# Transposes of two feature tiles' probabilities one step sooner in each half of the attention

## The chip, the cores and the metric

The kernel runs on one core of one Trainium2 chip. The metric is the device time of one execution in microseconds (us), as the median over several executions.

## What is computed

A decoder block for 256 tokens of width 1024, in float32. One normalised input is projected by `w_in` into seven parts; two gated mixers run side by side, a causal gMLP mixer (`y_a`) and an attention with 16 heads of 64 (`y_b`); they are merged, projected and added to the input. Two more stages follow, a squared-ReLU MLP and a gate on per-layer embeddings. With 256 tokens there is one block of keys, so the attention is plain causal attention with a bias by distance. Cut to what matters:

```python
h = rms_norm(x, norm_mix_g)
za_u, za_v, q, k, v_att, g_a, g_b = jnp.split(h @ w_in, offsets, axis=-1)
y_a = sgu_mixer(jax.nn.gelu(za_u), jax.nn.gelu(za_v), w_sgu_spatial, b_sgu_spatial, ln_v_g, ln_v_b)
y_b = moba_attention(heads(q), heads(k), heads(v_att), rel_bias)   # softmax(q k^T / 8 + bias, causal) @ v
merged = jax.nn.sigmoid(g_a) * y_a + jax.nn.sigmoid(g_b) * y_b
x = x + merged @ w_out
x = x + jnp.square(jax.nn.relu(rms_norm(x, norm_ffn_g) @ w_ff1)) @ w_ff2
x = x + jax.nn.sigmoid(rms_norm(x, norm_ple_g) @ w_ple_gate) * (p @ w_ple_proj)
return rms_norm(x, norm_final_g)
```

## The kernel before

**Weights.** All weights come as 1 MB tiles (128 x 2048) in one fixed order, through four buffers (`raw`). ScalarE rounds each tile into a high part `hi` (L85), VectorE takes the rest as a low part `lo` (L86), and TensorE multiplies the parts. Both parts have three buffers. A tile is split two tiles ahead of its use, and the load of a tile waits until the low part of the tile four before it has been taken.

**Attention, in two halves.** The features are worked on in eight feature tiles of 128 (two heads each), numbered `c` = 0 to 7; each half `J` of a Python loop handles four of them, in two pairs `a` and `b`. The order of the instructions on every engine is the order in which the code is written (a manual schedule); nothing is moved by a planner. One half runs through: `keys(a)`, `keys(b)` with the scores of the first two feature tiles in its middle, `att_normalise` of these two, the value projection `w_va` and the gate projection `gate_a`, into which the transposes (`att_transpose`) and the value products (`value_two`) of the first two feature tiles and the scores and softmax of the third and fourth (`score_two`) are put as extra work. Then come `att_normalise` for the third and fourth, `gate_b(a)`, `merge_b(a)`, `gate_b(b)`, `merge(a)`. The value products of the third and fourth feature tile are made one stage later: in the middle of `keys` of the second half (`values_b(1)`), and after the first twelve matmuls of the output projection (`values_b(3)`).

**The lines at stake.** `att_transpose(c)` puts six transposes of the normalised probabilities `s` on TensorE (L428), written into the PSUM tile `sp` in which the scores had been, and one ScalarE copy of all six to SBUF, `pt` (L429). `att_values(c)` multiplies `pt` with the values into the one PSUM buffer `yb` (L440, L442). `gate_b(j)` is a projection of two PSUM tiles, each of 16 matmuls (L215, L217) and followed by a ScalarE copy (L229); then VectorE adds two halves (L232) and scales (L473), and ScalarE takes the tanh `tb` (L475). Its optional `mid` is extra work that is issued after the first PSUM tile's copy. `merge(j)` transposes four blocks of `u` (L485), and VectorE and ScalarE write the merged features `mT` (L486, L108, L109).

**PSUM.** The `sp` tiles have two buffers of two banks each. After the loop that pool is closed, and the four accumulators `o` of the output projection take its place (L121, L123, L124: 12 matmuls for each 128 rows of `w_out`, six for each half of the columns). So the first matmul of the output projection has to wait until the last `sp` tile has been read, which the copy L429 of feature tile 7 does. In the built program that first matmul waits for ScalarE alone, and the count that it waits for is that of this copy.

Of the kernel before, what the change touches and what calls it, by code (L numbers as in the profile page):

```python
# [51 lines left out]
def block_kernel(ctx: ExitStack, tc: tile.TileContext, xt, xk, pt, rows, wst, bsp, rel, buckets, wts, out):  # L52
# [43 lines left out]
    def weights(key, width, ahead=3):  # L96
        i = POS[key]
        split_to(i + ahead)
        k = 2048 // width
        return (hi[i].rearrange("p (k c) -> p k c", k=k), lo[i].rearrange("p (k c) -> p k c", k=k))  # L100
# [28 lines left out]
    def bank(tag="mm", bufs=3, shape=(P, 2, 256)):  # L129
        return ps.tile(list(shape), F32, tag=tag, name=f"{tag}_t", bufs=bufs)  # L130
# [77 lines left out]
    def two_rows(R):  # L208
        return R[:, None, :].to_broadcast([P, 2, S])

    def wide_mm(o, wh, wl, x, f, ks):

        fs = slice(f * P, (f + 1) * P)
        for k in ks:
            nc.tensor.matmul(o, wh[:, k, fs], x[:, k], start=k == 0, stop=False, skip_group_check=True)  # L215
        for k in ks:
            nc.tensor.matmul(o[:, 0], wl[:, k, fs], x[:, k, 0], start=False, stop=k == KD - 1, skip_group_check=True)  # L217

    def wide_out(name):
        return act.tile([P, 2, 2, S], F32, tag="ln", name=name, bufs=2)  # L220

    def proj_T(key, x, mid=None):

        wh, wl = weights(key, CW)
        z = wide_out(f"z_{key[0]}{key[1]}")
        for f in range(2):
            o = bank()
            wide_mm(o, wh, wl, x, f, range(KD))
            nc.scalar.activation(z[:, f], o, AF.Copy)  # L229
            if f == 0 and mid:  # L230
                mid()
        nc.vector.tensor_add(z[:, :, 0], z[:, :, 0], z[:, :, 1])  # L232
        return z[:, :, 0]

    def proj_tok(name, c, post, mids={}):


        os_ = [bank(shape=(P, 512)) for t in range(2)]
        for i in range(2):
            wh, wl = weights((name, 2 * c + i), 512)  # L240
            for t in range(2):
                ts = slice(t * P, (t + 1) * P)
                for k in range(4):
                    kk = 4 * i + k
                    nc.tensor.matmul(os_[t], xg2[:, kk, 0, ts], wh[:, k], start=kk == 0, stop=False)  # L245
                    nc.tensor.matmul(os_[t], xg2[:, kk, 0, ts], wl[:, k], start=False, stop=False)  # L246
                    nc.tensor.matmul(os_[t], xg2[:, kk, 1, ts], wh[:, k], start=False, stop=kk == KD - 1)  # L247
                if i:
                    post(t, os_[t])
                for f in mids.get(2 * i + t, ()):  # L250
                    f()
# [82 lines left out]
    def by_token(dst, c, func):  # L334
        def post(t, o):
            nc.scalar.activation(dst[:, t, halves(c)], o, func, scale=r0[:, t:t + 1])
        return post
# [74 lines left out]
    def att_normalise(c):  # L412
        s, sm = sc_sb[c]
        rc = small.tile([P, 2, 2], F32, tag="rc", name=f"rc{c}")
        nc.vector.reciprocal(rc, sm)
        for i, cs in enumerate(parts):
            for h in range(2):
                nc.vector.tensor_scalar(s[:, h, cs], s[:, h, cs], rc[:, i, h:h + 1], 0.5,
                                        op0=OP.mult, op1=OP.mult)

    def att_transpose(c):

        s, _ = sc_sb.pop(c)
        pp = sp_.pop(c)
        pt_sb[c] = tmp.tile([P, 2, 3, P], F32, tag="pt", name=f"pt{c}", bufs=2)
        for h in range(2):
            for d, src in ((0, 256), (1, 0), (2, 128)):
                nc.tensor.transpose(pp[:, h, d * P:(d + 1) * P], s[:, h, src:src + P], ident)  # L428
        nc.scalar.activation(pt_sb[c][:, :, :, ::-1], pp[:, :, :RVW].rearrange("p h (d s) -> p h d s", d=3), AF.Copy)  # L429
# [14 lines left out]
    def keys(j, mid=None):  # L444
        o = proj_T(("w_qk", 4 + j), xg2, mid)
        nc.vector.tensor_tensor(kT[:, 2 * j:2 * j + 2], o, two_rows(R0), op=OP.mult)

    def score_two(c):

        for i in range(2):  # L450
            score_mm(c + i)
        for i in range(2):
            softmax(c + i)

    def value_two(j):
        for i in range(2):
            att_values(2 * j + i)
# [3 lines left out]
    def gate_a(J, mids):  # L461

        def post(t, o):
            th = tmp.tile([P, 512], F32, tag="th", name=f"ta{J}{t}", bufs=3)
            nc.scalar.activation(th, o, AF.Tanh, scale=rh[:, t:t + 1])
            ut = u[:, t, halves(J)]
            nc.vector.scalar_tensor_tensor(ut, th, 1.0, ut, op0=OP.add, op1=OP.mult)

        proj_tok("w_ga", J, post, mids)

    def gate_b(j, mid=None):
        z = proj_T(("w_gb", j), xg2, mid)
        nc.vector.tensor_tensor(z, z, two_rows(R0), op=OP.mult)  # L473
        tb[j] = tmp.tile([P, 2, S], F32, tag="th", name=f"tb{j}", bufs=3)
        nc.scalar.activation(tb[j], z, AF.Tanh, scale=0.5)  # L475

    def merge_b(j):
        nc.vector.scalar_tensor_tensor(tb[j], tb[j], 1.0, yb[j], op0=OP.add, op1=OP.mult)

    def merge(j):  # L480

        o = bank()
        for k in range(2):
            for t in range(2):
                nc.tensor.transpose(o[:, k, t * P:(t + 1) * P], u[:, t, (2 * j + k) * P:(2 * j + k + 1) * P], ident)  # L485
        nc.vector.scalar_tensor_tensor(tb[j], o, 0.5, tb[j], op0=OP.mult, op1=OP.add)  # L486
        split_act(mT[:, 2 * j:2 * j + 2], tb[j])

    def values_b(j):
        value_two(j)  # L490
        merge_b(j)

    for J in range(2):
        a, b, c = 2 * J, 2 * J + 1, 4 * J
        keys(a, mid=(lambda: values_b(a - 1)) if J else None)
        if J:
            merge(a - 1)
        keys(b, mid=lambda: score_two(c))
        att_normalise(c)
        att_normalise(c + 1)  # L500
        proj_tok("w_va", J, by_token(va, J, AF.Copy), {2: (lambda: att_transpose(c),)})
        gate_a(J, {0: (lambda: att_transpose(c + 1),), 1: (lambda: value_two(a),), 2: (lambda: score_two(c + 2),)})
        att_normalise(c + 2)
        att_normalise(c + 3)
        gate_b(a)
        merge_b(a)
        gate_b(b, mid=lambda: att_transpose(c + 2))
        merge(a)
        att_transpose(c + 3)


    late = act.tile([P, 4, D], F32, tag="TB", name="late")
# [363 lines left out]
```

## Time and profile before

| | us |
|---|---|
| median of 3 runs | 432.77 |
| lowest and highest of the 3 | 432.01 and 433.40 |
| the profiled execution | 432.29 |
| its span, first to last instruction | 430.6 |

In the span TensorE (PE) is busy for 97%, VectorE (DVE) for 66%, ScalarE (ACT) for 56%; TensorE's granted clock is 0.993 of full speed in the mean. A row of a timeline has start, duration, engine, line, operation, tile written and tiles read, shapes, count, and in brackets the idle time before it with what ended it. Matmuls are pipelined, so rows of PE overlap: the time from one row's start to the next one's is what a group of matmuls takes, and the duration holds the drain as well.

### The profile page before, as it was taken

The numbers are of one execution on the slowest core, as the hardware profiler recorded it, in microseconds if no ns is written. First come the engines' busy times: TensorE is split into PE (matmuls) and PEld (weight loads), VectorE is DVE, ScalarE is ACT, GpSimd is POOL, SyncE is SP. The second block draws the span as 40 slices with busy tenths as digits, with TensorE's granted clock in tenths as the row PEclk, the third lists the DMA queues.
The fourth block names the chain that finished last, engine by engine and source line by source line (L and its number), as shares of the span: only waits on it lengthen the run. The fifth ranks groups of instructions, "written<-read, shape, count | busy, mean of one in ns | idle before, by whom it ended". The sixth has DMA issues, their size and how long they took to land.

```text
span 430.6 us, 5546 instructions
## 1 busy us (share of the span) xinstructions
PE 416.6 (97%) x2188; PEld 352.5 (82%) x2188; DVE 285.1 (66%) x390; ACT 240.4 (56%) x369; POOL 10.4 (2%) x19
## 2 busy tenths in 40 slices
PE   8999999999999999969999999999999999999993
PEld 7888798888787887847888888888888888888882
DVE  3678958676677795774477876666666666646555
ACT  5695445585566673662356657555555555434824
POOL 1012010000000000000000000000000000000001
PEclk9999999999999999989999999999999999999998
DMA  8999685535424437263432766655554555452002
GB/s 273 421 393 387 243 280 209 191 103 196 195 88 137 167 125 267 74 269 129 164 110 99 281 243 211 240 184 185 184 187 181 188 191 189 187 205 90 0 2 98
DMA packets 13578, 81.45 MB, mean 189 GB/s; under 512 B 1557, under 2 KB 1829, under 8 KB 4976
## 3 DMA queue, kind: packets, MB, share of 16 engines
q1 hardware_dynamic: 12240, 77.60, 48.9%
q0 software_dynamic: 880, 2.97, 2.0%
q10 hardware_dynamic: 432, 0.54, 0.4%
q8 instruction: 17, 0.28, 0.3%
q14 instruction: 9, 0.07, 0.0%
HBM read 80.02 MB, written 1.07 MB: 188 GB/s over the span
## 4 chain that ended last, share of the span: by engine, by line
PE 86%; ACT 6%; DVE 5%; issue 2%; DMA 1%; POOLq 0%; POOL 0%; ACTq 0%
PE mm_t L215 20%; PE mm_t L217 10%; PE y L121 7%; PE y L124 7%; PE y L123 7%; PE mm_t L245 5%; PE mm_t L247 5%; PE mm_t L246 5%; PE o L121 2%; PE vo L123 2%; PE o L123 2%; PE o L124 2%; PE vo L121 2%; ACT s L408 2%; PE vo L124 2%
## 5 line engine op out<-in xcount | busy, mean ns | idle before, releaser
L86 DVE TENSOR_TENSOR lo<-raw,hi 128x1024 fp32r<-128x1024 f32 (+1 forms) x140 | 163.7, 1212 | 43.5 <-ACT hi L85 43.4
L85 ACT ACTIVATE hi<-raw 128x1024 fp32r<-128x1024 f32 (+1 forms) x140 | 138.1, 1037 | 41.3 <-PE o L124 8.2
L215 PE MATMUL mm_t<-xs,hi 128*128 128x512 f32 x248 | 62.4, 392 | 0.0
L215 PEld LDWEIGHTS mm_t<-xs,hi 128*128 128x128 f32 x248 | 45.2, 189 | 8.4
L215 PE MATMUL mm_t<-xg,hi 128*128 128x512 f32 x192 | 49.2, 398 | 0.0
L215 PEld LDWEIGHTS mm_t<-xg,hi 128*128 128x128 f32 x192 | 34.6, 189 | 7.3 <-issue 0.8
L245 PE MATMUL mm_t<-hi,xg 128*128 128x512 f32 x96 | 38.3, 399 | 0.0
L247 PE MATMUL mm_t<-hi,xg 128*128 128x512 f32 x96 | 37.5, 391 | 0.0
L246 PE MATMUL mm_t<-lo,xg 128*128 128x512 f32 x96 | 37.5, 390 | 0.0
L217 PEld LDWEIGHTS mm_t<-xs,lo 128*128 128x128 f32 x248 | 34.2, 190 | 2.7
L583 ACT ACTIVATE z<-mm_t 128x512 f32<-128x512 f32 x31 | 18.1, 594 | 32.1 <-PE mm_t L217 32.1
L217 PE MATMUL mm_t<-xs,lo 128*128 128x256 f32 x248 | 35.1, 282 | 0.0
L602 DVE TENSOR_TENSOR z<-z 128x512 f32<-128x512 f32 x16 | 11.1, 691 | 29.2 <-ACT z L583 29.2
L217 PEld LDWEIGHTS mm_t<-xg,lo 128*128 128x128 f32 x192 | 26.2, 190 | 2.0
L217 PE MATMUL mm_t<-xg,lo 128*128 128x256 f32 x192 | 26.8, 282 | 0.0
L124 PE MATMUL y<-hi,fs 128*128 128x512 f32 x64 | 25.0, 390 | 0.0
L123 PE MATMUL y<-lo,fs 128*128 128x512 f32 x64 | 25.0, 390 | 0.0
L245 PEld LDWEIGHTS mm_t<-hi,xg 128*128 128x128 f32 x96 | 18.0, 188 | 4.0 <-issue 0.3
L247 PEld LDWEIGHTS mm_t<-hi,xg 128*128 128x128 f32 x96 | 18.0, 188 | 3.8
L246 PEld LDWEIGHTS mm_t<-lo,xg 128*128 128x128 f32 x96 | 18.1, 188 | 3.4
L229 ACT ACTIVATE z_w_qk<-mm_t 128x512 f32<-128x512 f32 x16 | 9.5, 593 | 18.9 <-PE mm_t L217 14.8
L121 PE MATMUL y<-hi,fs 128*128 128x512 f32 x64 | 19.8, 391 | 0.0
(196 smaller groups left out, 620.9 us busy)
## 6 DMA issues: line engine op xcount, KB each, us to landing
raw<-wts SPq DMA_DIRECT2D x67, 1024.0 KB, 4.8
TB<-rvd POOLq DMA_DIRECT2D x1, 2048.0 KB, 11.5
raw<-wts SPq DMA_DIRECT2D x4, 256.0 KB, 5.2
raw<-wts SPq DMA_DIRECT2D x2, 512.0 KB, 6.6
xtok<-xk SPq DMA_DIRECT2D x2, 512.0 KB, 9.9
late<-xk SPq DMA_DIRECT2D x2, 512.0 KB, 6.3
out<-ots SPq DMA_DIRECT2D x3, 256.0 KB, 2.1
xg<-xt SPq DMA_DIRECT2D x1, 512.0 KB, 7.3
```

Source lines behind the costliest of these rows:

```text
L85: nc.scalar.activation(hi[i][:, s], raw[i][:, s], AF.Copy)
L86: nc.vector.tensor_tensor(lo[i][:, s], raw[i][:, s], hi[i].bitcast(F32)[:, s], op=OP.subtract)
L121: nc.tensor.matmul(os_[t], x[:, 0, ts[t]], wh, start=first, stop=False)
L123: nc.tensor.matmul(os_[t], x[:, 0, ts[t]], wl, start=False, stop=False)
L124: nc.tensor.matmul(os_[t], x[:, 1, ts[t]], wh, start=False, stop=last)
L215: nc.tensor.matmul(o, wh[:, k, fs], x[:, k], start=k == 0, stop=False, skip_group_check=True)
L217: nc.tensor.matmul(o[:, 0], wl[:, k, fs], x[:, k, 0], start=False, stop=k == KD - 1, skip_group_check=True)
L245: nc.tensor.matmul(os_[t], xg2[:, kk, 0, ts], wh[:, k], start=kk == 0, stop=False)
L246: nc.tensor.matmul(os_[t], xg2[:, kk, 0, ts], wl[:, k], start=False, stop=False)
L247: nc.tensor.matmul(os_[t], xg2[:, kk, 1, ts], wh[:, k], start=False, stop=kk == KD - 1)
L583: nc.scalar.activation(z[:, f], o, AF.Copy)
L602: nc.vector.tensor_add(z[:, :, 0], z[:, :, 0], z[:, :, 1])
```

## The change

`gate_b` gets a second optional piece of extra work, `end`, issued right after the projection's last instruction (the VectorE add L232) and ahead of its own scaling and tanh. The transposes of the third feature tile of a half move from the middle of `gate_b(b)` to the end of the projection in `gate_b(a)`, those of the fourth from behind `merge(a)` to the middle of `gate_b(b)`. Nothing is added or left out. No DMA moves.

```diff
-    def gate_b(j, mid=None):
+    def gate_b(j, mid=None, end=None):
         z = proj_T(("w_gb", j), xg2, mid)
+        if end:
+            end()
         nc.vector.tensor_tensor(z, z, two_rows(R0), op=OP.mult)
...
-        gate_b(a)
+        gate_b(a, end=lambda: att_transpose(c + 2))
         merge_b(a)
-        gate_b(b, mid=lambda: att_transpose(c + 2))
+        gate_b(b, mid=lambda: att_transpose(c + 3))
         merge(a)
-        att_transpose(c + 3)
```

TensorE's order from `gate_b(2)` to the output projection in the second half; `sp6` and `sp7` are the third and fourth feature tile's PSUM tiles, `hi26` and `lo26` the parts of the weights of `gate_b(2)`, `hi27` and `lo27` those of `gate_b(3)`, `hi28` the first tile of `w_out`. Before:

```order
L215 MATMUL mm_t_1576<-xg2_123,hi26_1420 128x512 x8
L217 MATMUL mm_t_1576<-xg2_123,lo26_1421 128x256 x8
L215 MATMUL mm_t_1608<-xg2_123,hi27_1469 128x512 x8
L217 MATMUL mm_t_1608<-xg2_123,lo27_1470 128x256 x8
L428 MATMUL sp6_1490<-ident_106,s6_1500 128x128 x6
L215 MATMUL mm_t_1634<-xg2_123,hi27_1469 128x512 x8
L217 MATMUL mm_t_1634<-xg2_123,lo27_1470 128x256 x8
L485 MATMUL mm_t_1656<-ident_106,u_313 128x128 x4
L428 MATMUL sp7_1495<-ident_106,s7_1511 128x128 x6
L121 MATMUL o00_1680<-hi28_1551,mT_713 128x512
```

And in the changed kernel:

```order
L215 MATMUL mm_t_1576<-xg2_123,hi26_1420 128x512 x8
L217 MATMUL mm_t_1576<-xg2_123,lo26_1421 128x256 x8
L428 MATMUL sp6_1490<-ident_106,s6_1500 128x128 x6
L215 MATMUL mm_t_1616<-xg2_123,hi27_1469 128x512 x8
L217 MATMUL mm_t_1616<-xg2_123,lo27_1470 128x256 x8
L428 MATMUL sp7_1495<-ident_106,s7_1511 128x128 x6
L215 MATMUL mm_t_1642<-xg2_123,hi27_1469 128x512 x8
L217 MATMUL mm_t_1642<-xg2_123,lo27_1470 128x256 x8
L487 MATMUL mm_t_1664<-ident_106,u_313 128x128 x4
L121 MATMUL o00_1680<-hi28_1551,mT_713 128x512
```

Each set of six transposes stands 16 matmuls earlier, the second of them ahead of the transposes of `u` as well; the matmul that opens the output projection follows the transposes of `u` directly.

ScalarE's order over the same place; `pt6` and `pt7` are the copies of the transposes, `z_w_gb` the copies of the gate projection, `tb` its tanh, `hi29` and `hi30` the high parts of the second and third tile of `w_out`. Before:

```order
L229 ACTIVATE z_w_gb2_1557<-mm_t_1576 128x512
L475 ACTIVATE tb2_1596<-z_w_gb2_1557 128x512
L85 ACTIVATE hi29_1601<-raw29_1418 128x1024 x2
L229 ACTIVATE z_w_gb3_1607<-mm_t_1608 128x512
L429 ACTIVATE pt6_1626<-sp6_1490 128x6x128
L229 ACTIVATE z_w_gb3_1607<-mm_t_1634 128x512
L475 ACTIVATE tb3_1654<-z_w_gb3_1607 128x512
L108 ACTIVATE mT_713<-tb2_1596 128x2x256
L429 ACTIVATE pt7_1664<-sp7_1495 128x6x128
L85 ACTIVATE hi30_1686<-raw30_1467 128x1024 x2
```

And in the changed kernel:

```order
L229 ACTIVATE z_w_gb2_1557<-mm_t_1576 128x512
L429 ACTIVATE pt6_1595<-sp6_1490 128x6x128
L477 ACTIVATE tb2_1604<-z_w_gb2_1557 128x512
L85 ACTIVATE hi29_1609<-raw29_1418 128x1024 x2
L229 ACTIVATE z_w_gb3_1615<-mm_t_1616 128x512
L429 ACTIVATE pt7_1634<-sp7_1495 128x6x128
L229 ACTIVATE z_w_gb3_1615<-mm_t_1642 128x512
L477 ACTIVATE tb3_1662<-z_w_gb3_1615 128x512
L108 ACTIVATE mT_713<-tb2_1604 128x2x256
L85 ACTIVATE hi30_1686<-raw30_1467 128x1024 x2
```

The copy `pt7` takes the place that `pt6` had, three instructions sooner, and `pt6` goes ahead of the tanh `tb2`. The first half moves in the same way, with feature tiles 2 and 3. VectorE's order stays as it was.

## Rows read from the trace of the kernel before

**Rows 1.** Page, busy time, share of the span and instructions by engine

```profile
PE 416.6 (97%) x2188; PEld 352.5 (82%) x2188; DVE 285.1 (66%) x390; ACT 240.4 (56%) x369; POOL 10.4 (2%) x19
```

**Rows 2.** Waits of PE over the whole span: total us, times, longest us

```profile
PE o L121 <- ACT pt L429: 4.3, 1, 4.3
...
PE yb_t L440 <- ACT pt L429: 0.7, 1, 0.7
```

**Rows 3.** Timeline of PE, end of the second half and output projection: start, duration

```profile
177.97 2.00 PE L215 MATMUL mm_t<-xg,hi 128*128 128x512 f32 x8
...
180.76 0.82 PE L428 MATMUL sp<-ident,s 128*128 128x128 f32 x6
181.34 2.10 PE L215 MATMUL mm_t<-xg,hi 128*128 128x512 f32 x8
...
184.66 0.82 PE L428 MATMUL sp<-ident,s 128*128 128x128 f32 x6
189.75 1.22 PE L121 MATMUL o<-hi,mT 128*128 128x512 f32 x2 [4.27 <-ACT pt L429]
...
192.48 0.70 PE L121 MATMUL o<-hi,mT 128*128 128x512 f32 x2
...
194.03 0.66 PE L440 MATMUL yb_t<-pt,va 128*64 128x256 f32 x4
...
195.53 0.73 PE L121 MATMUL o<-hi,mT 128*128 128x512 f32 x2
...
204.32 0.62 PE L121 MATMUL o<-hi,mT 128*128 128x512 f32 x2
```

**Rows 4.** Timeline of PE, value products in the keys of the second half

```profile
132.79 0.66 PE L440 MATMUL yb_t<-pt,va 128*64 128x256 f32 x4
...
134.33 0.66 PE L440 MATMUL yb_t<-pt,va 128*64 128x256 f32 x4 [0.67 <-ACT pt L429]
...
135.14 2.12 PE L215 MATMUL mm_t<-xg,hi 128*128 128x512 f32 x8
```

**Rows 5.** Timeline of ACT, end of the second half

```profile
182.09 0.63 ACT L475 ACTIVATE tb<-z_w_gb 128x512 f32<-128x512 f32 x1 [3.32 <-DVE z_w_gb L473]
182.63 1.99 ACT L85 ACTIVATE hi<-raw 128x1024 fp32r<-128x1024 f32 x2
184.53 0.58 ACT L229 ACTIVATE z_w_gb<-mm_t 128x512 f32<-128x512 f32 x1
185.00 0.80 ACT L429 ACTIVATE pt<-sp 128x768 f32<-128x768 f32 x1
...
188.37 0.63 ACT L108 ACTIVATE mT<-tb 128x512 fp32r<-128x512 f32 x1
188.91 0.79 ACT L429 ACTIVATE pt<-sp 128x768 f32<-128x768 f32 x1
```

**Rows 6.** Timeline of DVE, end of the second half

```profile
176.26 1.01 DVE L418 TENSOR_SCALAR s<-s,rc 128x256 f32<-128x256 f32 x4
...
189.03 0.69 DVE L109 TENSOR_TENSOR mT<-tb,mT 128x512 fp32r<-128x512 f32 x1 [0.70 <-ACT mT L108]
190.68 2.36 DVE L86 TENSOR_TENSOR lo<-raw,hi 128x1024 fp32r<-128x1024 f32 x2 [0.95 <-ACT hi L85]
```

**Rows 7.** Windows: length, busy us of PE, PEld, DVE, ACT, POOL; granted clock, DMA share, GB/s

```profile
122.00:132.00 10.00, 10.00 (x65) 8.96 (x65) 8.66 (x13) 5.16 (x8) 0.00 (x0) 1.00 0.34 111
132.00:134.30 2.30, 1.66 (x16) 1.16 (x14) 1.60 (x3) 1.89 (x4) 0.00 (x0) 1.00 0.91 353
...
185.50:189.75 4.25, 0.00 (x0) 0.00 (x0) 3.24 (x5) 2.71 (x6) 0.00 (x0) 0.94 1.02 388
189.75:192.50 2.75, 2.75 (x7) 2.17 (x8) 1.82 (x2) 1.84 (x2) 0.00 (x0) 0.50 0.18 74
```

**Rows 8.** Waits, the row of weight splits that waited for a load

```profile
ACT hi L85 <- DMA raw<-wts: 5.3, 5, 2.3
```

## The prediction

> **What bounds the kernel now.** I read the page's row of engines first: PE is busy for 97% of the span [rows 1], so most of the kernel can only be shortened by taking work off PE, and this change takes none off. What is left to win is PE's idle time, so the list of PE's own waits came next. Only two entries in it lie behind the first six microseconds, and both end with the ScalarE copy of the transposed probabilities, L429: 4.3 us ahead of the output projection's first matmul and 0.7 us ahead of a value product [rows 2]. These are the two places that the change touches. Then I read the timelines of PE, ACT and DVE around each of them, and the granted clock by windows.
>
> At the end of the second half PE issues the last six transposes at 184.66; six of them take 181.34 - 180.76 = 0.58 us until the next matmul may start, so PE could go on at 184.66 + 0.58 = 185.24. It starts the output projection at 189.75 [rows 3]. The copy that it waits for runs from 188.91 to 189.70. ACT did not wait for the transposes there: the copy stood in ACT's order behind the tanh of the gate and a rounding of the merged features, and ran as soon as the latter let it, 188.37 + 0.63 less the overlap of neighbouring instructions [rows 5]. So the wait is one of order on ACT. The gap has a second price. TensorE's granted clock is 0.94 over it and 0.50 behind it, that is 1.2 in place of 2.4 GHz [rows 7], and the first six matmuls of the output projection take 192.48 - 189.75 = 2.73 us [rows 3].
>
> In the keys of the second half the same thing happens on a small scale: the second pair of value products starts at 134.33 with 0.67 us of idle time before it [rows 4], and the clock stays at 1.00 [rows 7].
>
> **The change, part by part.** It moves two sets of six transposes and two copies in each half; the count of instructions, their shapes and the loads stay. Times below are on the axis of the trace of before; what the first half gains shifts all that comes later by the same amount.
>
> *End of the second half, the copy.* In the changed order `pt7` stands where `pt6` stood on ACT, behind the first copy of `gate_b(3)`. That slot ran at 185.00 for 0.80 us [rows 5]. What comes ahead of it on ACT keeps its times: the tanh at 182.09 waits for VectorE with 3.32 us of idle time before it [rows 5], and the copy `pt6`, 0.80 us, now falls into that idle time. Its input is there: the transposes of feature tile 6 now run on PE at 177.97, where the first matmul of `gate_b(3)` ran [rows 3], and last 0.58 us. Those of feature tile 7 run one stage of 16 matmuls later, by 181.3 + 0.6 = 181.9, three microseconds ahead of their copy. So `pt7` ends at 185.80. Before, the matmul started 189.75 - 189.70 = 0.05 us behind the copy; so it now starts at 185.85, which gains 189.75 - 185.85 = 3.90 us. PE has the same work before it in another order and would be free at 185.24, so 0.61 us of waiting stay.
>
> *End of the second half, the clock.* If the clock stays up over 0.61 us, the first six matmuls cost half of 2.73, and 1.37 us are gained. The nearest row says that it does: 0.67 us of idle time in the first half left it at 1.00 [rows 4, 7]. The bounds of this term are 0 and 1.37; I take 1.37 by that row.
>
> The Trainium skill (TensorE: Matmul & The Clock Gate, Part 4: PE-mode transpose) says that transposes do not count as work for the clock in the way that matmuls do. By that page the stretch that looks idle would be longer, with the four transposes of `u` in front of the wait; the trace here shows three sets of transposes between 122 and 132 at a clock of 1.00 [rows 7], none of them next to a wait. The case that it would make is the first rival below.
>
> *First half.* The second pair's copy moves up in the same way, by 188.91 - 185.00 = 3.91 us in the pattern of the second half, and the wait before it was 0.67 us, so it goes whole. The two pairs took 135.14 - 132.79 = 2.35 us [rows 4]; without a wait two pairs take 195.53 - 194.03 = 1.50 us [rows 3]. That gains 0.85 us; the wait's own entry gives 0.67 as the lower bound. I take 0.85, since starts on PE are what the next group follows.
>
> *What the moved work is moved past.* On PE the transposes of the third feature tile come 16 matmuls sooner and need the normalised probabilities. VectorE finishes them at 176.26 + 1.01 = 177.27 [rows 6], and PE gets there at 177.97 [rows 3]: 0.70 us of room. The fourth's are normalised about 1.1 us after that and asked for three microseconds later. Behind the transposes on PE stand the matmuls of `gate_b(b)`; these and their copies come 0.58 us later, and ACT takes the second copy only after `pt`, where it stood before. SP's and POOL's queues see nothing of it, as no DMA is issued by the moved code.
>
> *Whether the gain lasts.* What could be late next is the third tile of `w_out`. Its low part is ready at 190.68 + 2.36 = 193.04 [rows 6], even a little sooner once the copy no longer stands ahead of its high part on ACT; PE wants it at 204.32 [rows 3], so at about 199.1 after the shift of 5.27. That leaves 6 us. The weights themselves are not late: ACT waited five times for a load, 5.3 us in all [rows 8], and the same line comes out for the first 60 us alone. From the output projection on PE has no wait in the list [rows 2], so the shift is carried to the end.
>
> *Sum.* 3.90 + 1.37 + 0.85 = 6.12 us. The profiled execution took 432.29 us, so 426.17. It lies 0.48 us below the median of the runs shown, 432.77; from the median the sum gives 426.65. I put the forecast between them, at 426.4.
>
> **The rivals.**
>
> *The clock falls all the same.* The wait of 0.61 us stays, with the transposes of `u` right ahead of it, and the clock goes to 1.2 GHz for the same six matmuls. Then the gain is 3.90 + 0.85 = 4.75 and the time 427.5 from the profiled execution, 428.0 from the median. Against it stands the clock of 1.00 over 0.67 us of idle time [rows 7]; for it, that this one row is all there is, and that it has no transposes beside it.
>
> *The wait is on something else.* In the trace of before the end of the copy (188.91 + 0.79 = 189.70) [rows 5] and the end of VectorE's writing of the merged features (189.03 + 0.69 = 189.72) [rows 6] lie 0.02 us apart, so by time alone either could have released the matmul at 189.75. Were it the merged features, the change would not do what it says at the large place: they keep their time, the gap and the low clock stay, and 0.85 us is all, so 431.4. Against it: the first matmuls read features that were merged in the first half, and in the built program the first matmul waits for ACT alone, at the count of the copy.
>
> *Given back behind it.* The output projection and its residual could run into a wait that the gap had hidden, such as the splits of the fourth tile of `w_out`, which follow PE through the three buffers. Giving back 2 us would leave 428.2. The 6 us of room above speak against it.
>
> *Slower: PE stalls at the new place.* If the normalised probabilities came later than PE, PE would stand still ahead of all of `gate_b(b)`, in both halves. The room is 0.70 us. Each half then loses what the probabilities are late by, less 0.70; the gain of 6.12 is eaten at 3.06 us a half, so from 3.76 us of lateness on, and at 5 us the time would be 432.29 - 6.12 + 2 x 4.30 = 434.8. For that VectorE would have to put the split of a weight tile (2.36 us) [rows 6] and more ahead of the normalising. Its order is not changed, and it has the normalising ahead of that split.
>
> **How the numbers follow.** Forecast, 426.4: 0.84. Clock falls, 427.5 to 428.0: 0.06. Given back, 428.2: 0.04. Wait on something else, 431.4: 0.03. Slower, 434.8: 0.03. The runs before spread from 432.01 to 433.40; less 6.12 that is 425.9 to 427.3. Half a microsecond below it for bounds that I took too low, and the rival of the clock above it, give a range of 425.4 to 427.9. A difference of 0.3% (1.3 us) is about what can be told from no change. Forecast, clock and given back lie beyond that on the faster side, 0.94; the wait on something else lies at 0.3% with its 1.4 us and counts as no difference, 0.03; slower 0.03.
>
> **What would show it.** Right: in the list of PE's waits the value product's entry is gone and the output projection's is 0.3 to 0.6 us; the time from the copy `pt7` to the first matmul is 0.05 us; the windows show a clock of 1.00 through the start of the output projection; the two pairs of value products take 1.50 us. Wrong: a wait of PE for VectorE at L428; a clock of 0.50 behind the small gap; the first matmul starting at the end of the write to `mT`; a new entry in PE's list between the output projection and the end.

## The result and the profile after

| | before, us | after, us |
|---|---|---|
| median (4 runs each) | 432.96 | 426.38 |
| lowest and highest | 432.01, 433.40 | 426.29, 426.61 |
| the profiled execution | 432.29 | 426.61 |
| its span | 430.6 | 424.9 |

The ratio is 0.9852, with a 95% interval of 0.9834 to 0.9869: 6.58 us less by the medians, inside the forecast range and 0.02 us from the forecast. The prediction was right. That it came so close is partly luck, as one term was too small and the point chosen between two bases made up for it; this is shown below. The fourth execution of the kernel before moved its median from 432.77 to 432.96.

The page's row of engines, which answers to [rows 1]. PE has the same 2188 matmuls; its share rose by a point.

```profile
PE 415.8 (98%) x2188; PEld 352.6 (83%) x2188; DVE 284.6 (67%) x390; ACT 240.6 (57%) x369; POOL 9.7 (2%) x19
```

The list of PE's waits over the whole span, which answers to [rows 2] (total us, times, longest us). The value products' entry is gone, and that of the output projection fell from 4.3 to 0.4 us.

```profile
PE o L121 <- ACT pt L429: 0.4, 1, 0.4
```

PE's timeline at the end of the second half, which answers to [rows 3] (start, duration). The transposes L428 stand at 177.56 and 181.03, each directly behind a stage of 16 matmuls and without idle time ahead; the output projection starts at 185.45. L487 is the line that was L485 before, L477 was L475, and L475 was L473.

```profile
177.56 0.82 PE L428 MATMUL sp<-ident,s 128*128 128x128 f32 x6
...
181.03 0.82 PE L428 MATMUL sp<-ident,s 128*128 128x128 f32 x6
...
184.46 0.60 PE L487 MATMUL mm_t<-ident,u 128*128 128x128 f32 x4
185.45 0.73 PE L121 MATMUL o<-hi,mT 128*128 128x512 f32 x2 [0.39 <-ACT pt L429]
...
186.94 0.61 PE L121 MATMUL o<-hi,mT 128*128 128x512 f32 x2
...
188.40 0.66 PE L440 MATMUL yb_t<-pt,va 128*64 128x256 f32 x4
```

PE's timeline at the value products in the keys of the second half, which answers to [rows 4]. The two pairs follow each other without a gap.

```profile
133.23 0.66 PE L440 MATMUL yb_t<-pt,va 128*64 128x256 f32 x4
...
133.93 0.65 PE L440 MATMUL yb_t<-pt,va 128*64 128x256 f32 x4
...
134.73 2.11 PE L215 MATMUL mm_t<-xg,hi 128*128 128x512 f32 x8
```

ACT's timeline, which answers to [rows 5]. `pt6` runs at 178.48, in what had been idle time ahead of the tanh: the tanh now shows 2.40 us of it in place of 3.32. `pt7` runs at 184.60, behind the split of a weight tile and the first copy of `gate_b(3)`.

```profile
178.48 0.82 ACT L429 ACTIVATE pt<-sp 128x768 f32<-128x768 f32 x1
181.69 0.63 ACT L477 ACTIVATE tb<-z_w_gb 128x512 f32<-128x512 f32 x1 [2.40 <-DVE z_w_gb L475]
182.23 1.99 ACT L85 ACTIVATE hi<-raw 128x1024 fp32r<-128x1024 f32 x2
184.12 0.58 ACT L229 ACTIVATE z_w_gb<-mm_t 128x512 f32<-128x512 f32 x1
184.60 0.80 ACT L429 ACTIVATE pt<-sp 128x768 f32<-128x768 f32 x1
```

The normalising of the third feature tile on DVE, which answers to the first row of [rows 6]. It ends at 175.86 + 1.01 = 176.87, 0.69 us ahead of the transposes at 177.56. The last row below is VectorE's writing of the merged features, which answers to the second row of [rows 6]: it runs 3.19 us behind the start of the output projection at 185.45, so that start does not wait for it.

```profile
175.86 1.01 DVE L418 TENSOR_SCALAR s<-s,rc 128x256 f32<-128x256 f32 x4
...
188.64 0.69 DVE L109 TENSOR_TENSOR mT<-tb,mT 128x512 fp32r<-128x512 f32 x1 [0.70 <-ACT mT L108]
```

Two windows, one over the wait that is left and one over the twelve matmuls behind it, which answer to [rows 7] (length, busy us of PE, PEld, DVE, ACT and POOL, granted clock, DMA share, GB/s). The clock is 1.00 in both.

```profile
184.80:185.50 0.70, 0.31 (x4) 0.07 (x2) 0.70 (x1) 0.70 (x2) 0.00 (x0) 1.00 0.60 199
185.45:188.40 2.95, 2.95 (x13) 2.18 (x13) 2.20 (x4) 1.40 (x3) 0.00 (x0) 1.00 1.01 407
```

The terms of the sum, read from the two profiles:

| term | predicted, us | measured, us | how |
|---|---|---|---|
| first half | 0.85 | 0.85 | 2.35 before; 134.73 - 133.23 = 1.50 |
| start of the output projection | 3.90 | 3.89 | start 4.30 sooner, of which 0.41 came from ahead (177.97 to 177.56 for the same place in PE's work) |
| clock | 1.37 | 1.33 | twelve matmuls: 194.03 - 189.75 = 4.28 before, 188.40 - 185.45 = 2.95 after |
| sum | 6.12 | 6.07 | |

The spans differ by 5.7 us, less than the sum, because the profiled execution of after was 0.47 us behind already ahead of the first moved instruction: the first matmuls of `gate_b(0)` stand at 116.98 before and at 117.45 after, with the same work ahead of them. 6.07 - 0.47 = 5.60, which leaves 0.1 us. The two rows, before and after:

```profile
116.98 1.98 PE L215 MATMUL mm_t<-xg,hi 128*128 128x512 f32 x8
117.45 1.98 PE L215 MATMUL mm_t<-xg,hi 128*128 128x512 f32 x8
```

### The profile page after: what moved, and what is told of

It reads as the page before. It is cut to its first block, busy times and chain, and to the rows that moved or that the text cites. A ratio compares the mean times of both kernels' runs of the same rounds, so it can differ in the third digit from the quotient of the medians.

```text
span 424.9 us, 5547 instructions
## 1 busy us (share of the span) xinstructions
PE 415.8 (98%) x2188; PEld 352.6 (83%) x2188; DVE 284.6 (67%) x390; ACT 240.6 (57%) x369; POOL 9.7 (2%) x19
## 3 DMA queue, kind: packets, MB, share of 16 engines
HBM read 80.02 MB, written 1.07 MB: 191 GB/s over the span
## 4 chain that ended last, share of the span: by engine, by line
PE 90%; DVE 3%; ACT 3%; DMA 2%; issue 1%; SPq 0%; POOLq 0%; POOL 0%; ACTq 0%
PE mm_t L215 22%; PE mm_t L217 11%; PE y L121 7%; PE y L124 7%; PE y L123 7%; PE mm_t L245 5%; PE mm_t L247 5%; PE mm_t L246 5%; PE o L121 2%; PE o L123 2%; DMA raw<-wts 2%; PE o L124 2%; PE vo L123 1%; PE vo L124 1%; PE vo L121 1%
```

## The experiments

Each kernel was timed beside the kernel before. The first four shared 15 runs of it (median 432.87), the next two 9 runs (433.63).

**1. The first half alone.** Against the changed kernel:

```diff
-        gate_b(a, end=lambda: att_transpose(c + 2))
+        gate_b(a, end=(lambda: att_transpose(c + 2)) if J == 0 else None)
         merge_b(a)
-        gate_b(b, mid=lambda: att_transpose(c + 3))
+        gate_b(b, mid=lambda: att_transpose(c + 3 if J == 0 else c + 2))
         merge(a)
+        if J != 0:
+            att_transpose(c + 3)
```

> The change is made in the first half alone; the second half keeps its old order. Theory (two separate waits on the order of ScalarE, whose prices add up): the first half gives 0.85 us, the wait of 4.3 us ahead of the output projection and the low clock behind it stay, 432.1 us. Rival (the gain of the two halves hangs together, for instance since the weight loads or the buffers of the second half follow from the first): a gain clearly other than 0.85 us, or a wait ahead of the output projection other than 4.3 us.

Measured: 431.77 us, ratio 0.9973 (0.9961 to 0.9986), 1.1 us by the medians, with the expected 0.85 inside the interval. The value products take 134.18 - 132.68 = 1.50 us in its timeline, the wait ahead of the output projection is 4.3 us. The theory holds. One thing was not expected: in this profile the low clock covered all twelve matmuls ahead of the value products, not six, and they took 194.22 - 188.80 = 5.42 us.

```profile
132.68 0.66 PE L440 MATMUL yb_t<-pt,va 128*64 128x256 f32 x4
...
134.18 2.11 PE L215 MATMUL mm_t<-xg,hi 128*128 128x512 f32 x8
...
188.80 1.22 PE L121 MATMUL o<-hi,mT 128*128 128x512 f32 x2 [4.28 <-ACT pt L429]
...
194.22 0.81 PE L440 MATMUL yb_t<-pt,va 128*64 128x256 f32 x4
```

Windows of this kernel over these twelve matmuls, with the clock at 0.50 in both:

```profile
188.80:191.50 2.70, 2.70 (x6) 2.15 (x7) 1.78 (x2) 1.84 (x2) 0.00 (x0) 0.50 0.17 70
191.50:194.20 2.70, 2.70 (x7) 1.65 (x5) 0.59 (x1) 0.00 (x0) 0.00 (x0) 0.50 0.33 76
```

**2. The second half alone.** The same edit with `J == 1` in place of `J == 0` and `J != 1` in place of `J != 0`.

> The change is made in the second half alone. Theory: the wait of 0.67 us before the second pair of value products stays, the wait ahead of the output projection falls to about 0.4 us by the list of waits, the clock stays at 1.00, the gain is 3.9 + 1.3 = 5.2 us, 427.7 us. Rival: less than 4.5 us, were the clock's part not there without the first half's gain.

Measured: 427.19 us, ratio 0.9864 (0.9848 to 0.9880), 5.7 us by the medians. The list of PE's waits has both entries as expected:

```profile
PE yb_t L440 <- ACT pt L429: 0.7, 1, 0.7
PE o L121 <- ACT pt L429: 0.4, 1, 0.4
```

The two halves alone gain 1.1 and 5.7 us, the whole 6.6: within the intervals the prices add up, and neither half's gain needs the other's. 5.7 is more than the 5.2 expected, a second sign that the clock's term is larger than the profile of before shows; it is a weak one, as the interval reaches down to 5.2.

**3. The fourth tile's transposes one more place up.**

```diff
-        gate_b(a, end=lambda: att_transpose(c + 2))
+        gate_b(a, end=lambda: (att_transpose(c + 2), att_transpose(c + 3)))
         merge_b(a)
-        gate_b(b, mid=lambda: att_transpose(c + 3))
+        gate_b(b)
         merge(a)
```

> The fourth feature tile's transposes go up one more place, right behind the third's at the end of gate_b(a), so that both copies fall into the idle time of ScalarE ahead of the tanh. Theory (what is left ahead of the output projection is the copy's place behind the split of a weight tile and one copy of the gate on ScalarE): the rest of the wait goes, 0.6 us less than the changed kernel, 425.8 us, no wait of PE on ScalarE left in the list. Rival A: the probabilities of the fourth tile are normalised only 0.1 us ahead of the new place, so PE waits for VectorE there instead, 0.1 to 0.5 us a half, and nothing is won. Rival B: the wait ahead of the output projection stays, as it is for something else than the copy, 426.4 us.

Measured: 425.69 us (425.47 to 425.78), ratio 0.9829 (0.9814 to 0.9845), 0.7 us below the changed kernel, as the theory has it. On PE the twelve transposes follow each other, and the output projection starts right behind the transposes of `u`, with no wait:

```profile
177.03 1.47 PE L428 MATMUL sp<-ident,s 128*128 128x128 f32 x12
...
183.93 0.60 PE L487 MATMUL mm_t<-ident,u 128*128 128x128 f32 x4
184.28 0.71 PE L121 MATMUL o<-hi,mT 128*128 128x512 f32 x2
```

On ACT both copies run in the idle time ahead of the tanh, of which 1.70 us are left:

```profile
177.94 1.51 ACT L429 ACTIVATE pt<-sp 128x768 f32<-128x768 f32 x2
181.15 0.63 ACT L477 ACTIVATE tb<-z_w_gb 128x512 f32<-128x512 f32 x1 [1.70 <-DVE z_w_gb L475]
```

Rival A falls: there is no wait of PE for VectorE. Rival B falls: what the output projection waited for was the copy. This kernel beats both.

**4. The gap of the kernel before, filled.** Fourteen matmuls whose result nothing reads; against the kernel before, behind its last `att_transpose(c + 3)`:

```diff
+        if J == 1:
+            fill = bank()
+            for k in range(14):
+                nc.tensor.matmul(fill, xg2[:, 0, 0, :P], xg2[:, k % KD], start=True, stop=True)
```

> The kernel before, with 14 extra matmuls of 128x512 into a spare PSUM tile that nothing reads, right behind the last transposes, so that PE works for 3.2 of the 4.5 us of its gap. The output projection still starts when the copy is done. Theory (the low clock behind the gap is the price of PE's idle time): the clock is 1.00 behind the gap, the first six matmuls take 1.4 to 1.5 us in place of 2.73, and the time is 1.3 us below the kernel before, 431.6 us, though not a microsecond of the wait is gone. Rival (the low clock comes from something else at that place): the clock falls all the same, 432.9 us.

Measured: 431.00 us (430.85 to 431.22), ratio 0.9953 (0.9939 to 0.9966), 1.87 us below the kernel before, with 14 matmuls more. The output projection starts no sooner: at 190.01, 0.26 us later than in the profile of before, and this execution was 0.26 us behind already at `gate_b(0)` (117.24 against 116.98). PE's timeline has the filling at 185.50, 1.05 us of idle time behind it, and the first six matmuls take 191.51 - 190.01 = 1.50 us, with the granted clock at 1.00 from 185.50 to 193.00:

```profile
185.50 3.47 PE L513 MATMUL mm_t<-xg 128*128 128x512 f32 x14
190.01 0.73 PE L121 MATMUL o<-hi,mT 128*128 128x512 f32 x2 [1.05 <-ACT pt L429]
...
191.51 0.62 PE L121 MATMUL o<-hi,mT 128*128 128x512 f32 x2
```

So the low clock is the price of PE's idle time: the rival, something else at that place, falls. The experiment measures the clock's term by itself, and at 1.87 us (1.5 to 2.6 by the interval) that term is larger than the 1.33 of the profiled execution.

**5. The fourth tile's transposes only as far as the end of `gate_b(b)`.** Against the changed kernel:

```diff
-        gate_b(a, end=lambda: att_transpose(c + 2))
+        gate_b(a)
         merge_b(a)
-        gate_b(b, mid=lambda: att_transpose(c + 3))
+        gate_b(b, mid=lambda: att_transpose(c + 2), end=lambda: att_transpose(c + 3))
         merge(a)
```

> The third feature tile's transposes stay where they were before (middle of gate_b(b)); the fourth's go only as far as the end of gate_b(b), so their copy stands on ScalarE behind the second copy of gate_b(b) and ahead of the tanh. Theory: the copy runs at 186.2 to 187.0 on the axis of the kernel before, the output projection starts at 187.05, PE has 1.8 us without work. The first half's wait goes whole, 0.85 us. With the clock up over 1.8 us the gain is 2.7 + 1.3 + 0.85 = 4.9 us, 428.1 us; with the clock down behind it, 3.6 us, 429.4 us. Rival (what stands right ahead of the output projection on ScalarE does not matter, only the transposes' place on PE): the wait goes as in the changed kernel, 426.4 us.

Measured: 427.45 us, ratio 0.9867 (0.9848 to 0.9887), 1.07 us above the changed kernel. The rival falls: on PE the transposes stand at 183.34, well ahead, and the output projection waits for the copy on ACT, which ends at 185.27 + 0.82 = 186.09, 0.05 us ahead of the start. PE is without work from 183.99 + 0.35 = 184.34 to 186.14, the 1.80 us that were expected (0.35 us are what four such transposes take, see below). The last row is ACT's.

```profile
183.34 0.81 PE L428 MATMUL sp<-ident,s 128*128 128x128 f32 x6
183.99 0.60 PE L487 MATMUL mm_t<-ident,u 128*128 128x128 f32 x4
186.14 0.72 PE L121 MATMUL o<-hi,mT 128*128 128x512 f32 x2 [1.55 <-ACT pt L429]
...
185.27 0.82 ACT L429 ACTIVATE pt<-sp 128x768 f32<-128x768 f32 x1
```

The windows of the wait and of what follows show the clock at 1.00 over 1.55 us of idle time:

```profile
184.40:186.10 1.70, 0.19 (x2) 0.00 (x0) 1.45 (x2) 1.69 (x3) 0.00 (x0) 1.00 1.01 402
186.10:189.10 3.00, 2.96 (x12) 2.17 (x12) 2.01 (x5) 2.17 (x4) 0.00 (x0) 1.00 1.02 388
```

So all but 1.07 us of the gain comes without the third tile's move at all; and the expected 428.1, which priced the clock at 1.3 us, was 0.65 us too high.

**6. The third tile's transposes one more place up, too soon.** Against the changed kernel:

```diff
-        gate_b(a, end=lambda: att_transpose(c + 2))
+        gate_b(a, mid=lambda: att_transpose(c + 2))
```

> The third feature tile's transposes go up one more place, to the middle of gate_b(a); the fourth's stand as in the changed kernel. Theory (the room ahead of the normalised probabilities is 0.70 us in the changed kernel, and 16 matmuls take 2.8 us): PE waits for VectorE at L428 for about 2.1 us in each half; in the second half some 0.6 us of that comes out of the wait that is left ahead of the output projection, so the time is 3.5 us above the changed kernel, 429.9 us. Rival (PE's order has slack, and the wait on ScalarE alone sets the pace): as the changed kernel, 426.4 us.

Measured: 429.58 us, ratio 0.9918 (0.9902 to 0.9933), 3.2 us above the changed kernel where 3.5 were expected. PE waits for VectorE ahead of the transposes in each half, and no longer for ScalarE ahead of the output projection. The list of PE's waits, and the timeline of the second half:

```profile
PE sp L428 <- DVE s L418: 3.6, 2, 1.8
```

```profile
174.19 1.98 PE L215 MATMUL mm_t<-xg,hi 128*128 128x512 f32 x8
176.00 1.11 PE L217 MATMUL mm_t<-xg,lo 128*128 128x256 f32 x8
178.91 0.88 PE L428 MATMUL sp<-ident,s 128*128 128x128 f32 x6 [1.79 <-DVE s L418]
```

Sixteen matmuls of this shape take 2.79 us (177.97 to 180.76 in [rows 3]), so PE was at the transposes at 174.19 + 2.79 = 176.98 and lost 1.93 us in each half; 2 x 1.93, less the 0.64 us of waiting that it hides behind, is 3.2. The granted clock stays at 1.00 over this wait and behind it, from 176.90 to 182.40. This is the mechanism of the slower rival, with its price: the place that the change chose is 0.69 us from it.

**7 and 8. The kernel before, profiled again.**

> The kernel before, unchanged, profiled again. Theory (the stretch at 1.2 GHz behind the long gap is not of one length from run to run, and that is what spreads the times of before over 1.9 us where kernels without the gap spread over 0.3 us): the wait is 4.3 us again, and the low clock covers six to twelve matmuls behind it, 2.7 to 5.4 us, a cost of 1.3 to 2.7 us. Rival (the stretch is the same in every run, and the spread comes from the start of the kernel): six matmuls at the low clock again, 2.73 us.

> The same kernel as the run before this one, a further profile for the same question: the length of the stretch at 1.2 GHz behind the gap, 2.7 us if it is fixed, another length between 2.7 and 5.4 us if it is not.

Both have the wait of 4.3 us. PE's timeline of the first of the two, from the output projection's start through the sixth and the twelfth matmul:

```profile
189.81 1.22 PE L121 MATMUL o<-hi,mT 128*128 128x512 f32 x2 [4.27 <-ACT pt L429]
...
192.54 1.05 PE L121 MATMUL o<-hi,mT 128*128 128x512 f32 x2
...
195.08 0.66 PE L440 MATMUL yb_t<-pt,va 128*64 128x256 f32 x4
```

And of the second:

```profile
190.06 1.04 PE L121 MATMUL o<-hi,mT 128*128 128x512 f32 x2 [4.26 <-ACT pt L429]
...
192.60 1.05 PE L121 MATMUL o<-hi,mT 128*128 128x512 f32 x2
...
194.60 0.66 PE L440 MATMUL yb_t<-pt,va 128*64 128x256 f32 x4
```

The twelve matmuls take 195.08 - 189.81 = 5.27 and 194.60 - 190.06 = 4.54 us, against 4.28 in the profile that the prediction had, 5.42 in experiment 1, and 2.95 without the gap. The low clock thus cost 2.3, 1.6, 1.3 and 2.5 us in four executions, 1.9 in the mean, and the profile of before had the lowest of them. So the stretch is not the same in every run, and in this the rival falls. But the start of the kernel has a share of its own. The first matmuls of `gate_b(0)` in the two profiles:

```profile
117.05 1.98 PE L215 MATMUL mm_t<-xg,hi 128*128 128x512 f32 x8
117.31 1.98 PE L215 MATMUL mm_t<-xg,hi 128*128 128x512 f32 x8
```

Against the profile that the prediction had (116.98 there, 4.28 us for the twelve matmuls, 432.29 us in all), the first of the two is 0.07 us later here and 0.99 us longer in the twelve matmuls, and 1.04 us slower in all; the second is 0.33 us later and 0.26 us longer, and 0.60 us slower in all. The two shares account for both.

The times say the same. The two kernels with the long gap spread by 1.6 us (before, 432.28 to 433.92 in 15 runs) and 1.9 us (experiment 1, 431.36 to 433.27 in 10). Of the kernels whose clock stays up, the changed one and experiments 2, 3, 4 and 5 spread by 0.3 to 0.6 us in 4 or 5 runs each, and experiment 6 by 0.8 us in 5.

The granted clock over the whole span, which is on record for every execution, sorts the times of before: of the 15 executions, the eight at 0.986 or 0.987 took 432.87 to 433.92 us and the seven at 0.989 to 0.993 took 432.28 to 432.74; of the 9, the six at 0.987 took 433.20 to 433.93 and the three at 0.993 took 432.41 to 432.70. So the median of before hangs on how many of each kind fall into it: 432.96, 432.87 and 433.63 in the three sets here.

## Why the prediction was right, point by point

- **What bounded the kernel.** The two waits were the right places. Experiments 1 and 2 price them apart, and their gains add up to that of the whole.
- **The wait is one of order on ACT.** Right. The output projection started 0.05 us behind the copy before, as it does after (184.60 + 0.80 = 185.40, start at 185.45). In experiment 5 the copy stands elsewhere on ACT, and the start is again 0.05 us behind its end; in experiment 3 it stands far ahead, and no wait is left.
- **The waiting that stays.** 0.61 us were forecast; PE was free at 184.46 + 0.35 = 184.81 (the 0.35 are what four such transposes take elsewhere, 195.48 to 195.83 in the trace of after) and started at 185.45: 0.64. The list of waits has 0.39 for it, as it counts from the end of the row, 184.46 + 0.60 = 185.06.
- **The clock over the small wait.** Right: it stayed at 1.00, with the transposes of `u` right ahead of the wait. This closes the first rival. The Trainium skill (TensorE: Matmul & The Clock Gate, Part 4: PE-mode transpose) says that transposes do not count as busy time in the way that other work does; no run here shows an effect of that. In experiment 5 ten transposes and the wait behind them fill the time from 183.34 to 186.14, 2.80 us, and the clock behind it is 1.00.
- **The size of the clock's term.** Here the working was too small. 1.37 us came from one execution, [rows 3], and was called the upper bound of the term. By four profiles the mean is 1.9, and by experiment 4 it is 1.87. The prediction saw the other end of this, the 0.48 us by which the profiled execution lay below the median, and split the difference without knowing its cause; that is the lucky part. From the median, the sum with 1.9 in place of 1.37 gives 432.96 - 3.90 - 1.9 - 0.85 = 426.3, against 426.38. For executions like the profiled one 1.37 was about right: from 432.61, the median of the seven executions with the higher clock, the forecast sum of 6.12 gives 426.5.
- **First half.** 0.85, to the last digit of the profile.
- **The wait on something else.** The 0.02 us between two candidate ends could not decide; the built program's wait could. The trace of after confirms it, where the merged features are written from 188.64 on and the output projection starts at 185.45.
- **Given back behind it.** Nothing was: from the output projection on PE has no entry in its list of waits in the trace of after.
- **The slower rival.** It did not come, with 0.69 us of room against 0.70 forecast. Experiment 6 uses the room up and shows the price.

## What to carry to other kernels

When an engine waits, look whether the instruction that releases it was itself ready and only stood late in its own engine's order: moving it into that engine's idle time cost nothing here, as its input was ready, and how far it may go was read from the row that makes the input. Move on until the next wait shows: one place further won another 0.7 us for the fourth tile, and lost 3.2 us for the third. A term that comes from the clock behind a long wait should not be taken from one execution; a spread of the times that is wider than that of like kernels is a sign of it.

## What the runs showed of the hardware

The stretch at 1.2 GHz behind one and the same gap of 4.3 us of idle time was not of one length: 12 matmuls took 4.28, 4.54, 5.27 and 5.42 us in four executions, against 2.95 at 2.4 GHz. Gaps of 0.39 (after), 0.67 (before, first half), 1.05 (experiment 4), 1.55 (experiment 5) and 1.79 us (experiment 6) left the clock at 1.00. And work that nobody needs made the kernel faster: 14 matmuls in the gap, whose result nothing reads, were worth 1.87 us.
